# A rotation kernel limited by its transfers: stores of 1 MB on one queue, and half of the loads on a second queue

## The chip, the cores and the metric

The kernel runs on one core of one Trainium2 chip. The metric is the device time of one execution in microseconds (us), lower is better. All runs told here are of the fast state, with a granted clock of 1.0. A difference of less than 2% counts as "the same"; most runs were timed in five rounds against the kernel before on the same chip.

## The reference

```python
def setup_inputs():
    batch, c, h, w = 32, 3, 256, 256
    return {"x": np.random.randn(batch, c, h, w).astype(np.float32)}

def reference(x):
    return np.rot90(x, k=-1, axes=(-2, -1)).astype(np.float32)
```

96 images of 256 x 256 float32 are turned by 90 degrees: 25.17 MB are read and 25.17 MB written.

## The kernel before

The images are cut into 12 slabs of 2 MB (2 x 4 images). A slab is loaded, transposed by VectorE in two instructions of 32 x 32 blocks, and stored. All 12 slabs stay in SBUF at once. VectorE writes the result of slab n into the place of slab n-1; slab 0 goes to PSUM, and ScalarE copies it to SBUF at the end. "Short" transfers have contiguous pieces of 8 KB (8 rows), "long" ones of 16 KB (16 rows). A slab with long loads has short stores, and the other way round.

```python
    RL, RS = 16, 8
    I = 2
    ...
    long_st = (0, 1, 2, last)
    ...
    for n in range(n_slabs):
        if n in (1, 2):
            ld = nc.sync.dma_start(out=units[n], in_=ld_short[n])          # 2 MB
            continue
        for i in range(I):                                                 # 1 MB each
            if n in long_st:
                ld = nc.sync.dma_start(out=units[n][:, i], in_=ld_short[n][:, i])
            else:
                ld = nc.sync.dma_start(out=units[n][i::I].rearrange("p i f -> p (i f)"), in_=ld_long[n, i])
            if (n, i) == (last, 0):
                mark = ld

    def store(n, t, i):                                                    # 1 MB
        if n in long_st:
            return nc.sync.dma_start(out=st_long[n, i], in_=t[i::I].rearrange("p i f -> p (i f)"))
        return nc.sync.dma_start(out=st_short[n][:, i], in_=t[:, i])

    for n in range(n_slabs):
        t_in, t_out = units[n], units[n - 1] if n else turned0
        ...                                       # two transposes t_in -> t_out on VectorE
        if n in range(5, last):
            nc.sync.dma_start(out=st_short[n], in_=t_out)                  # 2 MB
        elif n:
            for i in range(I):
                st = store(n, t_out, i)
                if (n, i) == (1, 0):              # the first store waits for a late load
                    tc.add_manual_dep(st.ins, mark.ins.name, ..., reason="stores after loads")

    for i in range(I):
        nc.scalar.copy(out=units[last][:, i], in_=turned0[:, i])
    for i in range(I):
        store(0, units[last], i)
```

## Time and profile before

| | before |
|---|---|
| time, median of 6 runs | 123.78 us (123.75 to 123.86) |
| span of the profiled run | 121.9 us |
| bytes moved | 50.33 MB, one queue, 40 transfers |
| VectorE | first transpose at 8.07, last ends at 101.4 us |
| first store issued | 59.63 us |

The lines of this profile stand in the prediction below. In the slices, a packet's bytes are counted where the packet starts.

### The profile page before, as it was taken

What the parts mean: (1) busy time and instruction counts of PE and PEld (TensorE: products, weight loads), DVE (VectorE), ACT (ScalarE), POOL (GpSimd) and SP (SyncE); (2) the same over time, 40 slices, a digit from 0 to 9 for tenths busy, and PEclk for the clock granted to TensorE, in tenths of its full rate; (3) what the DMA queues carried; (4) which work ended last, traced back from release to release, by engine and by line L of the source; (5) the groups of instructions that cost most, each with busy time, mean ns of one, the idle gap of its engine ahead of it and who ended that gap; (6) DMA issues with size and microseconds to landing.
All of it is one profiled execution on the core that took longest, in us unless ns stands there. A gap on an engine that the chain in (4) does not pass through costs nothing.

```text
span 121.9 us, 137 instructions
## 1 busy us (share of the span) xinstructions
DVE 92.9 (76%) x24; ACT 4.9 (4%) x3; POOL 0.2 (0%) x4
## 2 busy tenths in 40 slices
DVE  0039999999999999999999999999999992000000
ACT  0000000000000000000400000000000007400000
POOL 0000000000000000000000000000000000000000
DMA  3999999999999999999999999999999999999994
GB/s 86 430 430 430 427 433 430 430 430 430 430 430 430 430 430 430 430 430 390 427 468 430 430 390 430 430 430 430 411 419 419 427 419 419 414 427 473 425 419 188
DMA packets 5248, 50.33 MB, mean 413 GB/s; under 512 B 640, under 2 KB 640, under 8 KB 640
## 3 DMA queue, kind: packets, MB, share of 16 engines
q1 hardware_dynamic: 5248, 50.33, 98.1%
HBM read 25.17 MB, written 25.17 MB: 413 GB/s over the span
## 4 chain that ended last, share of the span: by engine, by line
DVE 44%; issue 29%; DMA 6%; DVEq 3%; ACT 2%; ACTq 1%; SPq 0%
DVE u L98 26%; DVE u L92 12%; DVE turned L92 6%; DMA u<-in_x_dram 6%; DVEq L138 3%; ACT u L110 2%; ACTq L138 1%; SPq L73 0%; DVEq L92 0%
## 5 line engine op out<-in xcount | busy, mean ns | idle before, releaser
L98 DVE STREAM_TRANSPOSE u<-u 128x2048 f32<-128x2048 f32 x16 | 62.4, 3947 | 0.3
L92 DVE STREAM_TRANSPOSE u<-u 128x2048 f32<-128x2048 f32 x6 | 23.4, 3984 | 0.1
L92 DVE STREAM_TRANSPOSE turned<-u 128x2048 f32<-128x2048 f32 x2 | 7.1, 3586 | 8.1 <-DMA u<-in_x_dram 8.1
L110 ACT COPY u<-turned 128x2048 f32<-128x2048 f32 x2 | 3.6, 1869 | 40.5 <-DVE u L92 40.5
L110 ACT ACT_TABLE_LOAD x1 | 1.3, 1283 | 59.6 <-DMA u<-in_x_dram 59.6
L127 POOL MEMSET const-bfloat16-1.0<- 128x1 bf16 x1 | 0.1, 102 | 0.0
L127 POOL MEMSET const-uint8-127<- 128x1 uint8 x1 | 0.1, 102 | 0.0
L127 POOL MEMSET const-float32-0.0<- 128x1 f32 x1 | 0.1, 99 | 0.2 <-issue 0.2
L127 POOL MEMSET const-float32-1.0<- 128x1 f32 x1 | 0.1, 99 | 0.0
## 6 DMA issues: line engine op xcount, KB each, us to landing
u<-in_x_dram SPq DMA_DIRECT2D x20, 1024.0 KB, 19.6
out_dram<-u SPq DMA_DIRECT2D x12, 1024.0 KB, 12.1
out_dram<-u SPq DMA_DIRECT2D x6, 2048.0 KB, 20.9
u<-in_x_dram SPq DMA_DIRECT2D x2, 2048.0 KB, 13.5
```

The costliest lines, as they stand in the source:

```text
L92: nc.vector.transpose(out=dst[:, cs], in_=src[:, cs])
L98: nc.vector.transpose(out=dst[:, cs], in_=src[:, cs])
L110: nc.scalar.copy(out=units[last][:, i], in_=turned0[:, i])
L127: nc = _bacc.Bacc("TRN2", target_bir_lowering=False, num_devices=1)
L138: with _tile.TileContext(nc) as tc:
```

## The change

The intent: all stores become 1 MB (six of 2 MB are cut in two), and the second load of slabs 1 to 10 is issued on ScalarE's queue, so that two queues load at once (slabs 1 and 2, so far one load of 2 MB each, get two loads for this).

```diff
     for n in range(n_slabs):
-        if n in (1, 2):
-            ld = nc.sync.dma_start(out=units[n], in_=ld_short[n])
-            continue
         for i in range(I):
+            queue = nc.scalar if i and 0 < n < last else nc.sync
             if n in long_st:
-                ld = nc.sync.dma_start(out=units[n][:, i], in_=ld_short[n][:, i])
+                ld = queue.dma_start(out=units[n][:, i], in_=ld_short[n][:, i])
             else:
-                ld = nc.sync.dma_start(out=units[n][i::I].rearrange("p i f -> p (i f)"), in_=ld_long[n, i])
+                ld = queue.dma_start(out=units[n][i::I].rearrange("p i f -> p (i f)"), in_=ld_long[n, i])
...
-        if n in range(5, last):
-            nc.sync.dma_start(out=st_short[n], in_=t_out)
-        elif n:
+        if n:
             for i in range(I):
                 st = store(n, t_out, i)
```

## The prediction

> **What bounds the kernel now.** I read the page's busy shares and slices first, then its queue table, to see which resource is full from one end to the other.
>
> ```profile
> span 121.9 us, 137 instructions
> DVE 92.9 (76%) x24; ACT 4.9 (4%) x3; POOL 0.2 (0%) x4
> ...
> DMA  3999999999999999999999999999999999999994
> GB/s 86 430 430 430 427 433 430 430 430 430 430 430 430 430 430 430 430 430 390 427 468 430 430 390 430 430 430 430 411 419 419 427 419 419 414 427 473 425 419 188
> ...
> q1 hardware_dynamic: 5248, 50.33, 98.1%
> HBM read 25.17 MB, written 25.17 MB: 413 GB/s over the span
> ```
>
> The DMA engines are at 9 tenths or more in every slice but the first and the last, and they are 98.1% busy over the whole span. 50.33 MB at the steady 430 GB/s take 50.33e6 / 430e3 = 117.0 us. The span is 121.9, so everything else (start, end, three shallow dips) is 4.9 us. The measured time, 123.8, is a constant 1.9 us above the span. VectorE has 24% of the span free.
>
> The page's chain names VectorE first, which misleads: the chain ends at an ACT copy at 105 us, and then only transfers are left. So I looked at when transfers are issued, in the timeline of SyncE's queue (start, duration, line, what, count).
>
> ```profile
> 0.73 0.88 SPq L73 DMA_DIRECT2D u<-in_x_dram  x2
> 1.65 1.19 SPq L69 DMA_DIRECT2D u<-in_x_dram  x2
> ...
> 59.63 3.97 SPq L81 DMA_DIRECT2D out_dram<-u  x4
> 63.71 5.16 SPq L82 DMA_DIRECT2D out_dram<-u  x4
> 68.97 24.96 SPq L101 DMA_DIRECT2D out_dram<-u  x6
> ...
> 101.40 5.57 SPq L81 DMA_DIRECT2D out_dram<-u  x4
> ```
>
> The loads fill the queue until about 60 us (25.17 MB at 430 is 58.5 us). The stores then have data waiting: at 59.63 VectorE has long finished the first slabs. Late in the run SyncE does wait for VectorE before each store, as its own list of waits says:
>
> ```profile
> SPq L101 <- DVE u L98: 20.8, 4, 7.4
> SPq L81 <- DVE u L92: 7.4, 1, 7.4
> ```
>
> These waits cost nothing yet, because the slices show full DMA during them: stores issued earlier are still in the queue. How much earlier is the slack that the change may eat, and it is worked out below. The chain and the timeline give VectorE's two ends:
>
> ```profile
> 1.19 6.78 DMA u<-in_x_dram
> ...
> 8.07 7.09 DVE turned L92 x2
> ...
> 101.41 1.87 ACT u L110
> 103.27 1.77 ACTq L138
> ```
>
> VectorE starts when slab 0 (2 MB, two loads) has landed at 7.97, then works without a gap, 7.85 us a slab, to 101.4. ScalarE's two copies follow, to 105.0, and the last two stores need them.
>
> **What the Trainium skill says.** "DMA: Bandwidth & Descriptors", section "Where 436 GB/s comes from", puts the ceiling of the 16 SBUF ports at 435.2 GB/s and a core's HBM share near 358. The trace shows 430 steady with one core at work: it agrees with the first and exceeds the second. At most 1.2% can be gained in rate. Section "Issuing engines are not separate DMA queues" says that transfers from the scalar and sync engines run on the same 16 engines and interleave, and that several issuers only save issue time. No part of the trace tests this yet, since one queue carries everything; the first loads are issued in 0.88 us for two, and a 1 MB transfer takes 2.44 us (1.0486 MB / 430), so issue time is not short. Section "Queues, rings and completion order" says each DMA engine takes turns between its queues a packet at a time. That decides how two load streams share, and no run here shows it yet.
>
> **The change part by part.**
>
> *Loads.* 22 load transfers become 24 (the two of 2 MB split); 10 of them move to ScalarE's queue, which has nothing else to do until 101 us. Bytes do not change. In the built program the first load on SyncE and the first on ScalarE have nothing to wait for, and at most 8 transfers are out at once over both queues, as before. With 8 MB out, some 19 us of work, neither engine's sequencer can let the DMA engines run dry. The first store still waits for the first load of the last slab; on SyncE it is the 13th of 14, and ScalarE's ten end earlier. So the stores start at about 59.6 as now.
>
> *What moves is the order of arrival.* Slab 0's two loads, on SyncE, no longer have the engines to themselves: the halves of slabs 1 and 2 on ScalarE's queue take turns with them, both in contiguous pieces of 8 KB (RS = 8 rows of 256 floats for each partition), so equal shares. Landing of the k-th MB is 7.97 - 2 x 2.44 = 3.09 us, plus 2.44 k. Slab 0 is complete at k = 4 instead of 2: 3.09 + 9.76 = 12.85. VectorE starts 4.9 us later. Slab 1's half on SyncE is its third MB. Meanwhile ScalarE's queue has come to slab 3, which is loaded in 16 KB pieces (RL = 16 rows); if turns are by piece, SyncE gets a third: k = 7, 20.2, against VectorE ready at 12.95 + 7.1 = 20.05. If turns are by bytes, k = 6, 17.7. Slab 2 comes at k = 10, 27.5, against 28.0; slab 3 at k = 12, 32.4, against 35.9. So VectorE loses 4.9 to 5.1 us at the start and nothing later, and ends at 106.3 to 106.5 instead of 101.4.
>
> *Does that reach the end?* The stores move 2 MB per 4.88 us from some 60.5 on, in slab order 1 to 11 and then 0. Slab 11's stores are reached at 60.5 + 10 x 4.88 = 109.3, slab 0's at 114.2. A transfer issued needs about 1.4 us to start; this is an estimate from the first load, issued at 0.73 and landed, without the time of its bytes, 2.4 us later, of which I put an end part of 1 us aside. Slab 11 is issued at 106.4 and can start at 107.8, 1.5 us in hand (6.5 now). Slab 0 waits for the copies: 106.4 + 3.64 + about 0.5 = 110.5, start 111.9, 2.3 us in hand. Earlier slabs have more (slab 10: 98.5 + 1.4 against 104.4). The delay is hidden, with little to spare: it costs 0.
>
> *Stores.* Six of 2 MB become twelve of 1 MB. SyncE issues six more, at 0.37 to 1.26 us each, while it has idle time (the 20.8 us of waits). Both halves of a slab still wait for both transposes, so nothing can be sent earlier. Each of the 8 additional transfers of the whole program adds a completion. If the whole shortfall of 430 against the skill's 435.2 were a per-transfer cost, it would be 2.439 - 2.409 = 0.03 us each, an estimate: 8 x 0.03 = 0.24 us, all on the full queue, so on the path.
>
> *Sum:* 123.8 + 0.0 (loads' order) + 0.0 (issue) + 0.24 (completions) = 124.0 us.
>
> **The rivals.**
>
> (a) *The tail runs dry.* If slab 0 came later than 12.85, or VectorE met more waits on SyncE's third and fourth MB, the 1.5 us in hand would go and each further us would be added to the end. For it: the margin at slab 11 falls from 6.5 to 1.5, and the turn-taking by piece brings slab 1 to within 0.2 us of need. Against it: VectorE needs 7.85 us a slab, and loads bring one in 4.88, so a late start is the only large loss. 2 us more delay would make it 124.5, 4 us more 126.5, the 2% line.
>
> (b) *Two streams are slower than one.* For it: two places in HBM are read in turn, and no trace shows the rate of that. Against it: pieces of 8 and 16 KB are long, and both streams are sequential. 420 instead of 430 GB/s over the 24 MB of shared loading is 59.9 - 58.5 = 1.4 us: 125.4. As the stores start after the loads, this would be paid in full.
>
> (c) *Two streams are faster*, filling gaps that one queue leaves between transfers. At most 435.2: 58.5 - 57.8 = 0.7 us, so 123.3. With the dips at slices 18 and 23 (390, about 9% of 3.05 us, 0.3 us each) also gone it would be 122.8, still within 2%. The dip at the turn from loads to stores comes from the wait on the last slab's load, which stays.
>
> **Range and chances.** 2% is 2.5 us. Faster by that would need 121.3, a span of 119.4: only 2.4 us above the pure transfer time at 430, while the start until slab 0's first bytes and the end already take about that. I give it 0.02. Slower by 2% needs (a) with 4 us, or (b) with 412 GB/s and less, or a mix: 0.09. The rest, 0.89, is the same. The range is 123.1 (rival c, most of it) to 125.6 (rival b, or a with 3 us).
>
> **What would show it.** Right: the first transpose starts at about 12.9; VectorE has no later gap over 0.5 us and ends near 106.4; two queues carry some 10.5 and 39.8 MB; the slices read 425 to 432 during loads and about 420 during stores; the first store is issued near 59.6; SyncE's waits for VectorE stay and DMA stays at 9. Wrong: slices under 8 tenths from 105 us on (rival a); load slices under 422 or a first store after 61 us (rival b); load slices of 434 and a first store before 59 (rival c). Stores of 1 MB with lower slices than the 419 of now would say that I mis-sized the completion.

## The result, and the profile after

The changed kernel took 124.03 us (median of 6 runs, 123.87 to 124.53) against 123.78 us for the kernel before (6 runs). The ratio is 1.0023, with a 95% interval of 1.0004 to 1.0041: the same, as predicted, and some 0.25 us slower. Ratios here are the mean time of one kernel's fast runs over that of the other's of the same rounds, so they are not quite the ratio of the medians.

The page of the changed kernel, the same lines as were shown of before:

```profile
span 122.3 us, 145 instructions
DVE 93.0 (76%) x24; ACT 4.9 (4%) x3; POOL 0.2 (0%) x4
...
DMA  4999999999999999999999999999999999999994
GB/s 83 410 429 429 439 429 439 423 412 429 429 429 429 429 429 429 429 429 421 415 450 429 429 402 423 429 429 418 410 426 429 415 418 410 429 426 469 423 412 198
...
q1 hardware_dynamic: 4448, 39.85, 77.9%
q10 hardware_dynamic: 928, 10.49, 20.5%
```

The DMA engines are as full as before. ScalarE's queue (q10) has taken the predicted 10.49 MB. Now the timeline (start, duration, engine, line, what, count):

```profile
0.73 1.97 SPq L71 DMA_DIRECT2D u<-in_x_dram  x4
0.74 0.89 ACTq L71 DMA_DIRECT2D u<-in_x_dram  x2
...
13.48 7.08 DVE L90 STREAM_TRANSPOSE turned<-u 128x2048 f32<-128x2048 f32 x2 [13.48 <-DMA u<-in_x_dram]
...
60.13 3.98 SPq L79 DMA_DIRECT2D out_dram<-u  x4
...
106.94 5.55 SPq L79 DMA_DIRECT2D out_dram<-u  x4
```

VectorE starts 5.4 us later than before (13.48 against 8.07) and is done 5.5 us later (106.94 against 101.40), and this is hidden: the slices late in the run do not fall. The first store is issued 0.5 us later, so the loss is already there before any store moves a byte.

To see where so little time goes, I added up the packets of the traces: at what time, from the span's start, had k MB (of 1.0486e6 bytes each) been moved? All traces have their first packet at 1.72 to 1.82 us.

| us at which k MB had been moved | 2 | 12 | 26 | 36 | 48 (end of data) |
|---|---|---|---|---|---|
| before | 7.58 | 32.12 | 66.49 | 91.01 | 120.77 |
| after | 7.83 | 32.53 | 66.92 | 91.42 | 121.19 |
| later by | 0.25 | 0.41 | 0.43 | 0.41 | 0.42 |

The whole loss of the profiled run is there after the 12th MB of loads, and 0.25 us of it after the second. The stores (the 25th to the 48th MB) cost nothing more, though there are six more of them. The prediction put its 0.24 us into the completions of the additional transfers. That does not fit, so I held two theories against each other.

- **Theory C** (the prediction's): each additional transfer costs 0.03 us of the full queue.
- **Theory S**: the stores are free; what is lost is lost at the start, where a second queue is opened.

### The profile page after: what moved, and what is told of

Same layout as the page of the kernel before. It is cut to its first block, busy times and chain, and to the rows that moved or that the text cites. A ratio compares the mean times of both kernels' runs of the same rounds, so it can differ in the third digit from the quotient of the medians.

```text
span 122.3 us, 145 instructions
## 1 busy us (share of the span) xinstructions
DVE 93.0 (76%) x24; ACT 4.9 (4%) x3; POOL 0.2 (0%) x4
## 3 DMA queue, kind: packets, MB, share of 16 engines
q10 hardware_dynamic: 928, 10.49, 20.5%
## 4 chain that ended last, share of the span: by engine, by line
DVE 41%; issue 26%; DMA 16%; DVEq 3%; ACT 2%; ACTq 1%
DVE u L96 26%; DMA u<-in_x_dram 16%; DVE u L90 15%; DVEq L134 3%; ACT u L106 2%; ACTq L134 1%
## 5 line engine op out<-in xcount | busy, mean ns | idle before, releaser
L90 DVE STREAM_TRANSPOSE turned<-u 128x2048 f32<-128x2048 f32 x2 | 7.1, 3586 | 13.5 <-DMA u<-in_x_dram 13.5
## 6 DMA issues: line engine op xcount, KB each, us to landing
out_dram<-u SPq DMA_DIRECT2D x24, 1024.0 KB, 12.5
```

Of the source, the lines that this page charges most:

```text
L90: nc.vector.transpose(out=dst[:, cs], in_=src[:, cs])
```

## The experiments

Each edit is shown against the kernel it starts from. Medians of "before" on the three chips used were 123.77, 123.84 and 123.86 us. Twelve kernels were run; all of them gave right results.

### Stores alone, loads alone, one queue

`a1_stores_only` is the kernel before with the stores of the change:

```diff
-        if n in range(5, last):
-            nc.sync.dma_start(out=st_short[n], in_=t_out)
-        elif n:
+        if n:
```

> The kernel before with only the stores split into 1 MB; the loads as before, on one queue. Theory C (the prediction's: each additional transfer costs 0.03 us of the full queue): +0.18 us for 6 additional transfers. Theory S (what the changed kernel lost, it lost at the start, where a second queue is opened; the stores are free): 0.0 us, at most 0.05 (6 x 9 ns, the length of a completion packet in the traces). Time from the 24th to the 48th MB moved: 59.2 us as in both traces.

Measured: 123.86 us, ratio 1.0008 (0.9995 to 1.0021). From the 24th to the 48th MB: 59.1 us.

`a2_loads_only` is the changed kernel with the stores of before:

```diff
-        if n:
+        if n in range(5, last):
+            nc.sync.dma_start(out=st_short[n], in_=t_out)
+        elif n:
```

> The changed kernel's loads on two queues, with the stores of before (six of 2 MB). Theory C: +0.06 us (2 additional transfers). Theory S: the whole of the changed kernel's loss, +0.25 to +0.4 us, with the first MB 0.25 us later after the first packet than in the kernel before (3.6 against 3.4 us). VectorE starts at about 13.4 us under both.

Measured: 124.10 us, ratio 1.0027 (1.0015 to 1.0040). VectorE starts at 13.24 us.

`a3_one_queue` is the changed kernel with all loads on SyncE's queue:

```diff
-            queue = nc.scalar if i and 0 < n < last else nc.sync
+            queue = nc.sync
```

> The changed kernel with every load on SyncE's queue: 48 transfers of 1 MB in one queue. Theory C: +0.24 us, as the changed kernel has the same number of transfers. Theory S: 0.0 us, at most 0.07 (8 x 9 ns). VectorE starts at 8.0 again.

Measured: 123.73 us, ratio 1.0002 (0.9988 to 1.0016). This kernel has the same 48 transfers of 1 MB as the changed one, and none of its loss. One figure warns, though: its first MB is done 3.55 us after the first packet, nearly as late as in a2_loads_only (3.58; before 3.37), with one queue.

What follows: the loss belongs to the loads on two queues (+0.33 us alone), not to the number or the size of the transfers. Theory C falls in its size. The traces name a smaller cost: each transfer ends with one 4-byte completion packet on each of the 16 engines, with a mean of 9 ns in the trace of before; 8 more make 0.07 us, below what these runs resolve.

### The second queue, opened later or for one load

`a4_scalar_late` lets ScalarE's queue start only when slab 0 has landed:

```diff
+    scratch = ...                                  # a tile of 16 columns
     for n in range(n_slabs):
+        if n == 1:
+            gate = nc.scalar.copy(out=scratch, in_=units[0][:, 1, :16])
         for i in range(I):
             queue = nc.scalar if i and 0 < n < last else nc.sync
...
+            if i and 0 < n < last:
+                tc.add_manual_dep(ld.ins, gate.ins.name, ..., reason="second queue after slab 0")
```

> The changed kernel, but ScalarE's queue starts only after slab 0 has landed (a copy of 16 columns of it on ScalarE goes ahead of its loads). Theory C: +0.24 us. Theory S, if opening a queue costs only while the engines have nothing else queued: 0.0 to +0.1 us; if the opening costs wherever it comes: +0.25 us. First transpose at 8.0; slab 1 may be some 1 to 2 us late for VectorE, which the slack should hide.

Measured: 123.46 us, ratio 0.9977 (0.9964 to 0.9989). This is faster than the kernel before by 0.3 us, which neither theory had said. The slab that came late for VectorE cost it a gap of 3.3 us, not 1 to 2, and that was hidden too.

`b4_one_scalar_load` leaves a single load on ScalarE's queue:

```diff
-            queue = nc.scalar if i and 0 < n < last else nc.sync
+            queue = nc.scalar if i and n == 1 else nc.sync
```

> The changed kernel with a single load, slab 1's second half, on ScalarE's queue. If what costs is the opening of a second queue while the engines start (theory S): the whole +0.25 to +0.33 us is here with one load; the first MB is done 0.15 us or more later after the first packet than in the kernel before. If the shared loading as such costs (rival: two streams are slower than one): at most a tenth of it, +0.03 us. VectorE starts about 2.5 us later than before.

Measured: 123.96 us, ratio 1.0011 (0.9999 to 1.0024), about +0.14 us. It lies between the two expectations. In the profile the start is as slow as with ten loads. These are windows from 1 to 4 us (start and end, length, busy time of three engines, clock, DMA share, GB/s) of the kernel before, the changed kernel, and b4_one_scalar_load:

```profile
1.00:4.00 3.00, 0.00 (x0) 0.00 (x0) 0.00 (x0) 1.00 0.66 218
```

```profile
1.00:4.00 3.00, 0.00 (x0) 0.00 (x0) 0.00 (x0) 1.00 0.77 199
```

```profile
1.00:4.00 3.00, 0.00 (x0) 0.00 (x0) 0.00 (x0) 1.00 0.78 199
```

With two queues the engines have moved less (199 against 218 GB/s). That they are busier meanwhile (0.77 and 0.78 against 0.66) is no mark of two queues: c2_earlier_store below, with one queue at the start, is as busy and has moved as much as the kernel before:

```profile
1.00:4.00 3.00, 0.00 (x0) 0.00 (x0) 0.00 (x0) 1.00 0.76 218
```

In the changed kernel the first packets of 8 KB take up to 1.2 us (on ScalarE's queue) and 1.5 us (on SyncE's), where 0.31 is usual. Summed over the 16 engines, what the packets of 8 KB that start before 6 us take beyond 0.31 us is 14 to 15 us in the four kernels that open two queues at the start, and 6 to 12.5 in the others. In a4_scalar_late, where the second queue opens into a stream that is already running, none of that queue's packets of 8 KB takes longer than 0.37 us. Over all traces, the second MB is done at 7.78 to 7.83 us in the four kernels that open two queues at the start (after, a2, b4, and c5 below), and at 7.53 to 7.75 us in the nine with one queue at the start whose first load is of 1 MB (c2 7.69 and a3 7.75 are the latest of them; b3 below, whose first load is of 2 MB, has 7.78 with one queue and is not comparable). On average the start takes about 0.2 us more. The two groups don't overlap, but only 0.03 us lie between them, one-queue kernels differ among themselves by 0.22, there is one profile per kernel, and the b4 run alone would not have shown it in time. That the loads on two queues cost time is shown by a2_loads_only; that it is the opening of the queue is what the traces suggest, and not shown.

### Why opening the queue late is faster than before

The fast kernel pointed at the stores. Between 80 and 108 us, where all kernels store 8 KB pieces of slabs 4 to 10, the window of the kernel before and that of a4_scalar_late read:

```profile
80.00:108.00 28.00, 21.30 (x6) 3.63 (x2) 0.00 (x0) 1.00 1.01 423
```

```profile
80.00:108.00 28.00, 24.65 (x7) 3.21 (x2) 0.00 (x0) 1.00 1.01 427
```

423 against 427 GB/s with the engines full in both. By the packets, pieces of 8 KB that start between 85 and 110 us take a mean of 314 ns in the kernel before and 309 in a4_scalar_late; all 24 MB of stores take 59.2 us in one and 58.7 in the other. Two differences could be behind it. One is ScalarE: its table load had moved from 59.6 us to the start (**theory T**). The other is the first store. With ScalarE's loads late, SyncE's own loads were done early, so the first store was issued at 57.26 us in place of 59.63 and stood in the queue behind the loads well before these ended (**theory J**).

`c1_early_table` is the kernel before with the small copy alone:

```diff
+    scratch = ...                                  # a tile of 16 columns
+        if n == 1:
+            nc.scalar.copy(out=scratch, in_=units[0][:, 1, :16])
```

> The kernel before plus the small copy on ScalarE after slab 0 that a4_scalar_late has: ScalarE's table load moves from 59.6 us to the start, nothing else changes. It tests why a4_scalar_late is 0.3 us faster than before. Theory T (the table load, or ScalarE's long wait behind it, disturbs the stores): 123.77 - 0.4 = 123.4 us, and packets of 8 KB after 77 us take 309 ns instead of 314. Theory J (the stores run faster because they were in the queue before the loads ended): no change, 123.8 us and 314 ns.

Measured: 123.85 us, ratio 0.9999 (0.9987 to 1.0012); the table load is at 0.72 us, the late pieces take 314 ns. Theory T falls.

`c2_earlier_store` is the kernel before with a different load for the first store to wait for:

```diff
-            if (n, i) == (last, 0):
+            if (n, i) == (last - 1, 1):
                 mark = ld
```

> The kernel before with the first store waiting for the last load of slab 10 in place of the first load of slab 11: the first store is issued some 2.4 us earlier, near 57.2, as in a4_scalar_late, so that it stands in the queue behind the loads. Theory J: 123.4 us, 8 KB packets late in the run at 309 ns. Theory T: no change, 123.8 us and 314 ns. A third way, that two queues or the VectorE phase make the stores of a4_scalar_late fast, also says no change.

Measured: 123.37 us, ratio 0.9965 (0.9951 to 0.9978). This is the fastest kernel, faster than both the kernel before and the changed one. Its timeline and its late window:

```profile
57.25 2.46 SPq L81 DMA_DIRECT2D out_dram<-u  x4
```

```profile
80.00:108.00 28.00, 21.38 (x6) 3.63 (x2) 0.00 (x0) 1.00 1.01 428
```

The late pieces take 309 ns, and the stores 58.7 us. Theory J holds: 0.47 us for a first store issued 2.4 us sooner (the eighth came 5.4 us sooner, at 62.17 us in place of 67.62), with nothing else changed in the code.

`c3_late_store` is a4_scalar_late with the opposite edit:

```diff
-            if (n, i) == (last, 0):
+            if (n, i) == (last, 1):
                 mark = ld
```

> a4_scalar_late with the first store waiting for the last load of slab 11, so it cannot stand in the queue behind loads: first store near 61 us. A gap of about 1 us in the transfers is expected under all theories. Theory J: packets of 8 KB late in the run go back to 314 ns, time 123.46 + 0.4 + 1 = 124.9. Theory T: they stay at 309 ns, time 123.46 + 1 = 124.5.

Measured: 123.87 us, ratio 1.0002 (0.9990 to 1.0015). The edit did not do what I had meant. The scheduler put a store without that wait, by the program slab 1's other one, ahead of the marked one. It was issued at 50.44 us and covered the gap that I had expected. The rest followed at 62.23, with one store (2.4 us of work) ahead of it, and the late pieces took 312 to 314 ns again. So one store that stands in the queue early is not enough; what more it takes, this run does not show.

`c5_after_earlier` is the changed kernel with the mark of c2_earlier_store (there this load is on ScalarE's queue):

```diff
-            if (n, i) == (last, 0):
+            if (n, i) == (last - 1, 1):
                 mark = ld
```

> The changed kernel with the first store waiting for ScalarE's last load (slab 10) in place of SyncE's load of slab 11: the first store is issued near 50.5 us and stands behind the loads in SyncE's queue. If the early store is worth 0.45 us whatever the loads do (theory J): 124.03 - 0.45 = 123.6 us, late 8 KB packets at 309 ns; the second queue's opening cost stays. If J needs the loads of one queue: 124.0 us.

Measured: 123.63 us, ratio 0.9979 (0.9965 to 0.9993), pieces at 309 ns, first store at 50.98 us. The gain is worth the same on top of the change (the changed kernel had 1.0023). The kernel is some 0.2 us slower than c2_earlier_store (ratios 0.9979 and 0.9965, whose intervals overlap), which would fit the cost of the second queue. Beside a4_scalar_late (0.9977), which has early stores too but opens the queue late, it is no slower that these runs could tell: the time does not say that it matters when the second queue opens. a4_scalar_late gained at the start (2nd MB at 7.57 us) and had lost it again by the 26th MB (66.75 us against 66.57 in c2_earlier_store).

`c6_no_store_wait` is the kernel before without the wait:

```diff
-                if (n, i) == (1, 0):
-                    tc.add_manual_dep(st.ins, mark.ins.name, ..., reason="stores after loads")
```

> The kernel before with the first store's wait on a late load taken out: the stores follow the loads in SyncE's program anyway, so the first is issued once a completion counter comes free, near 45 us, and stands behind all loads. Theory J: as c2_earlier_store, 123.4 us and 309 ns. A rival: an early store shares the engines with loads that VectorE needs, or the longer queue costs: 123.8 us or more.

Measured: 123.74 us (123.53 to 123.94), ratio 0.9989 (0.9975 to 1.0003), not clear of the kernel before. The stores behave as theory J says (309 ns, 58.7 us), but time is lost before: the 26th MB is moved at 66.76 us against 66.57 in c2_earlier_store (each is one profile; this one is of the fastest of six runs). Why stores from 44.98 us on should cost 0.2 us there is open.

In all 14 traces (the kernel before, the changed one and the twelve) the split is clean. Where the first two stores were issued by some 58 us (a4, c2, b3 below, c5, c6), the window from 80 to 108 us shows 427 to 429 GB/s. Where the stores, or all but one, were issued at 59.6 us or later (before, after, a1, a2, a3, b1, b4, c1, c3), the late 8 KB pieces take 312 to 315 ns. What happens in the DMA engines is not shown by these traces: the slow packets begin only some 10 to 20 us after the late issue and are spread over many packets: about half of the late pieces of the kernel before take a mean of 317 ns, and in c2_earlier_store all take 309. By then the two kernels issue alike: from the twelfth store on (77.88 us against 77.98) their stores are issued within 0.1 us of each other. So what differs at 80 to 108 us is left over from the turn, and not from what is being issued then. The condition is shown, its cause is not.

### Smaller stores still, and the slack

`b1_half_stores` is a1_stores_only with the stores of slabs 5 to 10 cut once more:

```diff
     def store(n, t, i):
+        if n in range(5, last):
+            for j in range(2):
+                st = nc.sync.dma_start(out=st_short[n][j::2, i], in_=t[j::2, i])
+            return st
```

> The kernel before with the six stores of 2 MB cut into 24 of 512 KB (every second partition each, still 8 KB pieces): 18 additional transfers, three times what a1_stores_only added. Theory C (0.03 us each): +0.54 us. Theory S (stores are free but for the 9 ns of a completion packet): +0.16 us. A rival: SyncE needs up to 1.25 us to issue a store and 512 KB last 1.22 us, so issue could become the bound: then 125 us or more, with slices under 9 tenths.

Measured: 124.24 us, ratio 1.0028 (1.0016 to 1.0041), +0.38 us, between the two theories. The two profiled runs differ by more, 0.56 us (spans of 122.48 and 121.93). In them the last byte is moved at 120.89 us, 0.12 us later than before, which is near what 18 completions of 9 ns make (0.16). The other 0.4 us lie between the last byte and the end of the span (1.59 us; 1.13 to 1.30 in all the others). I have no test of that part, and it stays open. Issue by SyncE did not become the bound, though it came near: from 82 us on a store was issued every 1.2 to 1.5 us without a break, and the DMA slices stayed at 9 tenths.

`b3_late_vector` is c2_earlier_store with slab 0 loaded third:

```diff
-    for n in range(n_slabs):                       # the loop of the loads
+    for n in [1, 2, 0, *range(3, n_slabs)]:
```

> c2_earlier_store with slab 0 loaded third, so that VectorE starts at about 17.9 us, 9.8 later than before. It tests the slack that the prediction worked out (VectorE may end up to 107.9 us before the end moves). Prediction's model: VectorE ends at 111.2; slab 11's stores start at 112.6 in place of 109.3: 123.8 + 3.2 = 127.0 us, with slices under 9 tenths at about 105 to 113 us. Rival: the slack is larger or VectorE is not on the path: 123.4 to 124.

Measured: 125.92 us, ratio 1.0164 (1.0148 to 1.0180), +2.1 us against the kernel before and +2.55 against c2_earlier_store, from which it was made. Two pieces of its timeline, and its windows at the place where the queue runs dry:

```profile
18.46 7.08 DVE L92 STREAM_TRANSPOSE turned<-u 128x2048 f32<-128x2048 f32 x2 [18.46 <-DMA u<-in_x_dram]
...
111.90 5.50 SPq L81 DMA_DIRECT2D out_dram<-u  x4
```

```profile
105.00:108.00 3.00, 3.00 (x2) 0.00 (x0) 0.00 (x0) 1.00 1.03 437
108.00:111.00 3.00, 3.00 (x2) 0.00 (x0) 0.00 (x0) 1.00 0.81 341
111.00:114.00 3.00, 0.88 (x1) 2.09 (x2) 0.00 (x0) 1.00 0.41 175
```

and the last two of these windows in the changed kernel:

```profile
108.00:111.00 3.00, 0.00 (x0) 2.58 (x2) 0.00 (x0) 1.00 1.04 434
111.00:114.00 3.00, 0.00 (x0) 0.00 (x0) 0.00 (x0) 1.00 1.04 440
```

In b3 the DMA share falls to 0.81 and 0.41. By its packets, nothing moves from 111.00 to 113.04 us: slab 11's stores are issued at 111.90, when VectorE has ended, and the first of their packets starts 1.14 us later. In the changed kernel the windows at the same place are full. So the model of the prediction is right in kind: VectorE's start is free until its end reaches the moment at which the queue comes to slab 11. The size is off: the prediction's terms made the queue idle for 3.3 us (109.3 to 112.6), and it was 2.04. VectorE ended 0.7 us later than expected and the stores started after 1.14 us in place of 1.4, but above all the queue came to slab 11 later than I had put it: the 44th MB is moved at 111.00 us here and at 110.93 in the kernel before, in place of 109.3 (the 24th at 61.57 in the kernel before, in place of 60.5). The changed kernel has its 44th MB at 111.36 us. With 1.14 us to start, its VectorE could have ended at 111.36 - 1.14 = 110.2 us. It ended at 106.94, so it had 3.3 us in hand, not 1.5.

## Why the prediction was right, and which term of it was not

- **The bound.** Right. The DMA engines stay at 9 tenths from the second slice to the last but one, and the time moved by 0.25 us only.
- **Loads, order of arrival.** Right. Slab 0 lands some 5 us later: predicted first transpose 12.95, measured 13.48; 0.25 us of the difference is the slower start. The taking of turns by piece shows in the trace too: between 13.5 and 20.1 us SyncE's queue starts 118 pieces of 8 KB and ScalarE's 110 of 16 KB, and SyncE's load that needs the completion counter of slab 1's first half was issued at 20.16 us (predicted landing 20.2; by bytes it would have been 17.7):

```profile
20.16 0.47 SPq L73 DMA_DIRECT2D u<-in_x_dram  x1
```

- **The tail (rival a).** Right that the delay is hidden; the slack was put at 1.5 us and is 3.3. b3_late_vector shows both the slack and what lies behind it.
- **Issue.** Right: 0.
- **Completions, 8 x 0.03 = 0.24 us.** This is the term that failed, though the sum was hit. The whole shortfall from 435.2 GB/s was charged to transfers, as an upper limit, and then used as the estimate. The completion packets take 9 ns each, so 0.07 us; a3_one_queue, with all 8 additional transfers, measured 0.0, and a1_stores_only +0.09 with an interval that reaches zero.
- **Two streams (rival b).** Two streams were not slower than one in the steady part: from the 2nd to the 26th MB a2_loads_only needs 58.87 us (66.65 - 7.78) and the kernel before 58.91. The sign that the prediction had named for it, load slices under 422, came up all the same (410 and 412 in the changed page, beside 439): slices of 3 us are too short for such a line. What the prediction lacked is a cost of loading on two queues: +0.33 us in a2_loads_only, of which the traces put some 0.2 at the start. It took the place of the 0.24 that were not there. That the two are of one size is chance.
- **Loss not fully placed.** The changed kernel's profile loses a further 0.16 us between the 2nd and the 12th MB. a2_loads_only has the same loads and does not show it (12th MB at 32.33, 0.21 later than before, against 0.41). The changed kernel's runs also spread most (123.87 to 124.53). On this stretch the changed kernel needs 24.70 us, and kernels with one queue and a first load of 1 MB need 24.51 to 24.68. I take it for variation from profile to profile, which no run here proves.
- **A gain that nobody looked for.** Rival (c) counted the wait of the first store as something that stays. It was the one thing worth changing: 0.47 us in c2_earlier_store.

## What to carry to other kernels

When one resource is full from end to end, read a change by what it does to that resource at the start, at the turn from loads to stores, and at the end; 8 more transfers cost this kernel nothing that could be measured, and a second issuer 0.2 to 0.3 us. A sum that comes out right does not prove its terms: cut the change into its parts and run each alone. And try to let stores stand in the queue some microseconds before the loads end (here 2.4 us earlier made all the stores together 0.9% faster, while 14.6 us earlier brought no gain in time that was clear), and check in the late windows, not in the total alone, that they run at full rate.

## What the Trainium skill lacked or had wrong

- "DMA: Bandwidth & Descriptors", section "Issuing engines are not separate DMA queues", says that a second issuer only saves issue time. It agrees with the runs in the stream itself (58.87 against 58.91 us for 24 MB). It lacks that loads on two queues can cost a little (a2_loads_only, +0.33 us), as it seems at the start (2nd MB at 7.78 to 7.83 us against 7.53 to 7.75), and that the data needed first then comes later: VectorE started 5.4 us later.
- "DMA: Bandwidth & Descriptors", section "Where 436 GB/s comes from", says that for transfers between HBM and SBUF the HBM side, near 358 GB/s for each core, is what binds (it adds that a measurement of 425 GB/s is near the fabric's rate). That it binds does not hold for one core that works alone, as here: it loaded at a steady 430 GB/s and stored at 420 to 429 late in the run, close to the page's 435.2.
- "DMA: Bandwidth & Descriptors", section "Queues, rings and completion order", says that an engine takes turns between queues by the packet. The runs agree, if a packet is a piece of the trace: a queue with pieces of 8 KB beside one with 16 KB gets about a third (118 pieces against 110 from 13.5 to 20.1 us). How these pieces relate to the page's descriptors is not shown.
- No page has it that stores run slower after they join the queue late: 8 KB pieces take 312 to 315 ns instead of 309 late in the run, and the 24 MB of stores 59.1 to 59.3 us instead of 58.7 to 58.8 (b3_late_vector, which runs dry, left out), when all stores but one at most are issued less than 2 us before the first 24 MB are moved, or later still. With two stores issued some 4 us before that, it did not happen. The cause is not known.
- No page has the time in ns that a trace's completion packet takes in the stream of a transfer: a mean of 9 ns on each of the 16 engines.
